# Moving the pool of weight slots to a 512-byte boundary of the storage, and four more dummy products in the router

## The chip, the core and the metric

The kernel runs on one core of a Trainium2 chip. Five engines work side by side on that core's on-chip storage: TensorE (PE in the profile; its weight loads are listed apart as PEld), VectorE (DVE), ScalarE (ACT), GpSimd (POOL) and SyncE (SP), which here only issues transfers. Sixteen DMA engines move data between the chip's main memory and the storage. [...]

The metric is the time of one execution in microseconds (us), the median of several.

## The reference

Two blocks run one after the other on 256 tokens of width 1024, in float32. The first block is adaptive normalization, grouped-query attention and spatial gating, and then an expert-choice feed-forward layer; the second is a latent-attention and sliding-window layer followed by a forgetting-attention layer. The part that matters here is the feed-forward layer of the first block:

```python
def expert_choice_ffn(h, w_router, w1, w3, w2):
    n, d = h.shape[1], h.shape[2]
    cap = CAPACITY_FACTOR * n // N_EXPERTS
    aff = jax.nn.softmax((h @ w_router).astype(jnp.float32), axis=-1)
    gate, idx = lax.top_k(jnp.swapaxes(aff, 1, 2), cap)
    xe = jax.vmap(lambda hb, ib: hb[ib])(h, idx)
    hid = jax.nn.silu(jnp.einsum('becd,edf->becf', xe, w1)) * jnp.einsum('becd,edf->becf', xe, w3)
    ye = jnp.einsum('becf,efd->becd', hid, w2) * gate[..., None].astype(h.dtype)
```

There are 16 experts. Each picks 32 of the 256 tokens (`cap`), and has three matrices of 8 MiB, so 384 MiB of expert weights are read once.

## The kernel before

**Storage.** `body` (L63 on) opens pools that are laid into the storage in the order in which they are opened: `consts` (L71), `big` (L72), `work`. `consts` holds the small tables and `xT` (the running activations, 8 KiB in each of 128 partitions). `big` holds 23 slots of 8 KiB in each partition (`NSLOT`); whatever is large lives in a slot: weight chunks `w`, split halves `hi` and `lo`, activations. In the built program the first slot starts at byte 20,768 of each partition, which is 288 bytes past a multiple of 512, and since a slot is 8,192 bytes every slot starts 288 bytes past such a multiple.

**Loads.** Every weight chunk of 1 MiB goes into one slot. `queue` writes the list of loads down in the order in which they are wanted; `pump` (L252) issues them on SP's queue, one after the other, as long as slots are free (less `keep`, a number that `hold` sets for each stage). A load into a slot waits on SP until the slot's last reader is done, and all loads behind it wait with it. A chunk of an expert's `w1`, `w3` or `w2` is 128 rows of 8 KiB that lie in one piece in the main memory and in the slot; a chunk of `w_in`, `o_w_in`, `w_out` and the like is 1,024 pieces of 1 KiB.

**The router, and what follows it.** All engines run their instructions in the order of the program text. After the output projection (`p_out`) TensorE computes router scores (`p_rl`) and sums of squares (`p_st`); VectorE makes the scale; then the softmax, a transpose (`p_af`), and the choice of 32 tokens for each expert, four rounds of three instructions on VectorE (L981 to L984). From the indices a one-hot matrix is built through a small product (`one_hots`: `diag` on VectorE, `p_ix` on TensorE, `oh` on VectorE). For expert 0, `before_first` gathers its tokens chunk by chunk with narrow products (`p_g`, 32 columns) between the products of `hidden` (`p_h`), which read the chunks of `w1` (first pass, k = 0 to 7) and then those of `w3` (second pass). Then `expert` does the second product (`p_y`) and adds the result back to `xT` (`p_sc`). After expert 0 the tokens of the other 15 experts are gathered at once (`p_g`, 480 columns, 32 records), and experts 1 to 15 follow. All products go through the helper at L134.

**Dummy products.** `busy(n)` (L885) multiplies `ones` with `xT` n times into a bank of its own that nobody reads. In the router it stands at two places: `busy(6)` (L955), ahead of the transpose `p_af`, and `busy(9)` (L977), between `p_yn` and `p_ix`, while VectorE chooses the tokens:

```python
    rows_out(3)
    free(yT_)
    busy(9)
    gv = small("gv", (16, 32), bufs=1)
    iv = small("iv", (16, 32), U32, bufs=1)
    for r in range(4):
        V.max(gv[:, 8 * r:8 * r + 8], afT)
        V.max_index(iv[:, 8 * r:8 * r + 8], gv[:, 8 * r:8 * r + 8], afT)
        if r < 3:
            V.match_replace(afT, gv[:, 8 * r:8 * r + 8], afT, -1.0)
```

Of the kernel before, what the change touches and what calls it, by code (L numbers as in the profile page):

```python
# [9 lines left out]
F32 = mybir.dt.float32  # L10
# [53 lines left out]
def body(ctx, tc, x, c, ctx_in, c_ctx, w_mod, b_mod, g_mix, g_ffn, w_in, q_gain, k_gain, v_gain,  # L64
# [3 lines left out]
    nc = tc.nc  # L68
    PE, V, S, G = nc.tensor, nc.vector, nc.scalar, nc.gpsimd

    consts = ctx.enter_context(tc.tile_pool(name="consts", bufs=1))  # L71
    big = ctx.enter_context(tc.tile_pool(name="big", bufs=1))  # L72
    work = ctx.enter_context(tc.tile_pool(name="work", bufs=1))
    psum = ctx.enter_context(tc.tile_pool(name="psum", bufs=1, space=bass.MemoryType.PSUM))
    dram = ctx.enter_context(tc.tile_pool(name="dram", bufs=1, space=bass.MemoryType.DRAM))
# [26 lines left out]
    def bank(name):  # L102
        n = banks_free.popleft()
        t = psum.tile([128, 512], F32, name=name, tag="P%d" % n)
        owner[id(t)] = (banks_free, n, t, name)
        return t

    def free(*ts):
        for t in ts:
            q, n, _, _ = owner.pop(id(t))  # L110
            q.append(n)
        pump()
# [14 lines left out]
    def small(name, shape, dt=F32, bufs=2):  # L127
        return work.tile(list(shape), dt, name=name, tag="sm_" + name, bufs=bufs)
# [4 lines left out]
    def mm(o, lhsT, rhs, start, stop):  # L133
        PE.matmul(o, lhsT, rhs, start=start, stop=stop, skip_group_check=True)  # L134
# [750 lines left out]
    def busy(n):  # L885

        if n:
            p = bank("p_busy")
            for _ in range(n):
                mm(p[:, 0:256], ones, xT[:, 0, :], True, True)  # L890
            free(p)
# [82 lines left out]

    rows_out(3)
    free(yT_)
    busy(9)  # L977
    gv = small("gv", (16, 32), bufs=1)
    iv = small("iv", (16, 32), U32, bufs=1)
    for r in range(4):  # L980
# [914 lines left out]
```

## Time and profile before

| | |
|---|---|
| median of 3 runs | 1402.29 us (1401.91 to 1405.15) |
| the profiled execution's own time | 1401.61 us |
| its span, first to last instruction | 1399.8 us |
| mean granted clock of TensorE | 0.854 |
| TensorE busy | 1094.4 us (78%) |
| VectorE busy | 450.3 us (32%) |
| ScalarE busy | 265.6 us (19%) |
| GpSimd busy | 113.7 us (8%) |
| bytes moved | 482.74 MB, 345 GB/s on the mean |

The busy shares are averages over stages with different limits. From about 250 to 1,119 us the experts' weights stream in; before that stand the first block's attention and the router, and after it the second block. The profile's slices (40 equal ones of 35 us), the chain of waits and the windows tell which limit holds where.

### The profile page before, as it was taken

Reading aid. Unit: us, or ns where it says so; the run is one execution under the profiler, and the core shown is the slowest. Engines: PE = TensorE matmul, PEld = TensorE weight load, DVE = VectorE, ACT = ScalarE, POOL = GpSimd, SP = SyncE. Lnnn points to the kernel's source line nnn. Section 1 sums busy time; section 2 is a strip of 40 time slices with the busy share of each in tenths; the row PEclk is TensorE's granted clock in tenths of the full one; section 3 lists DMA queues with packets and bytes.
Section 4 is the critical chain, followed back from the end, with each engine's and each line's share of the span. In section 5 each row is a group of like instructions: output and inputs, shape, how many; then the busy total and the mean of one; then the engine's idle time right before and its main releaser. Section 6 shows DMA issues by size and latency. Waiting matters only on the chain.

```text
span 1399.8 us, 16525 instructions
## 1 busy us (share of the span) xinstructions
PE 1094.4 (78%) x6685; PEld 516.1 (37%) x6685; DVE 450.3 (32%) x1096; ACT 265.6 (19%) x529; POOL 113.7 (8%) x65
## 2 busy tenths in 40 slices
PE   5999998976777676786767767676676878899988
PEld 2775943311111011110101111011110566799877
DVE  3747433201011010110101011010111568967984
ACT  3446310000000000000000000000000345555453
POOL 1000100000000000000000000000000332560420
PEclk9999969968778798877968879687897899999999
DMA  9995799999999999999999999999999971482320
GB/s 371 374 395 238 290 343 412 372 420 420 419 420 420 419 419 420 420 420 419 420 420 420 420 420 420 419 420 419 420 420 415 344 230 61 124 264 84 121 91 31
DMA packets 114684, 482.74 MB, mean 345 GB/s; under 512 B 8010, under 2 KB 61520, under 8 KB 63152
## 3 DMA queue, kind: packets, MB, share of 16 engines
q1 hardware_dynamic: 113504, 479.10, 85.9%
q0 software_dynamic: 848, 2.48, 0.5%
q8 instruction: 53, 0.87, 0.3%
q14 instruction: 23, 0.19, 0.0%
q10 hardware_dynamic: 256, 0.10, 0.0%
HBM read 480.59 MB, written 1.06 MB: 344 GB/s over the span
## 4 chain that ended last, share of the span: by engine, by line
DMA 59%; PE 18%; DVE 9%; issue 2%; ACT 2%; SPq 0%; DVEq 0%; ACTq 0%
DMA w<-in_w_dram 58%; PE p_aT L134 3%; PE p_h L134 2%; PE p_out L134 2%; PE p_oo L134 2%; PE p_g L134 2%; PE p_eo L134 1%; PE p_aN L134 1%; PE p_y L134 1%; DVE pr L1316 1%; PE p_gate L134 1%; DVE pr L1297 1%; DMA w<-in_e_w_in_dram 1%; DVE ogl L1383 1%; PE p_busy L134 1%
## 5 line engine op out<-in xcount | busy, mean ns | idle before, releaser
L134 PE MATMUL p_h<-w,xe 128*32 128x512 f32 x1920 | 356.0, 837 | 179.3 <-DMA w<-in_w_dram 179.3
L134 PE MATMUL p_y<-w,hidT 128*32 128x512 f32 (+1 forms) x1088 | 227.8, 622 | 64.6 <-DMA w<-in_w_dram 46.2
L134 PEld LDWEIGHTS p_h<-w,xe 128*32 128x32 f32 x1920 | 46.7, 125 | 469.6 <-DMA w<-in_w_dram 422.7
L1054 DVE TENSOR_TENSOR hid<-s,p_h 128x512 f32<-128x512 f32 x16 | 11.0, 688 | 506.8 <-issue 454.9
L161 POOL TENSOR_TENSOR lo<-w,hi 128x2048 fp32r<-128x2048 f32 (+2 forms) x20 | 87.0, 4354 | 1024.9 <-DMA w<-in_w_dram 924.2
L134 PEld LDWEIGHTS p_y<-w,hidT 128*32 128x32 f32 x1088 | 53.1, 115 | 246.0 <-issue 174.3
L1067 ACT ACTIVATE ysh<-p_y,ig 128x512 fp32r<-128x512 f32 (+1 forms) x34 | 22.3, 663 | 547.2 <-PE p_y L134 547.2
L1068 DVE SCALAR_TENSOR_TENSOR ysl<-p_y,ig,ysh 128x512 fp32r<-128x512 f32 (+1 forms) x34 | 24.3, 719 | 251.2 <-ACT ysh L1067 249.8
L160 ACT CAST hi<-w 128x2048 fp32r<-128x2048 f32 (+3 forms) x48 | 79.1, 1673 | 25.0 <-DMA w<-in_e_w_in_dram 20.6
L161 DVE TENSOR_TENSOR lo<-w,hi 128x2048 fp32r<-128x2048 f32 (+2 forms) x28 | 52.4, 1893 | 27.2 <-ACT hi L160 25.9
L1052 ACT ACTIVATE s<-p_h 128x512 f32<-128x512 f32 x16 | 9.6, 597 | 265.2 <-PE p_h L134 265.2
L1072 DVE SCALAR_TENSOR_TENSOR xT<-p_sc,m,xT 128x256 f32<-128x256 f32 x128 | 51.8, 475 | 4.0 <-PE p_sc L134 4.0
L134 PE MATMUL p_aT<-y2h,hi 128*128 128x256 f32 x128 | 36.7, 286 | 0.0
L134 PE MATMUL p_aT<-y2h,lo 128*128 128x256 f32 x128 | 36.3, 284 | 0.2 <-POOL lo L161 0.2
L134 PE MATMUL p_aT<-y2l,hi 128*128 128x256 f32 x128 | 36.3, 284 | 0.1
L1301 ACT ACTIVATE pr<-pr,st 128x128 f32<-128x128 f32 x64 | 28.5, 446 | 32.4 <-DVE st L1297 32.4
L134 PE MATMUL p_mod<-w,cm 128*32 128x512 f32 x192 | 27.9, 669 | 3.0 <-DMA w<-in_w_mod_dram 2.2
L1316 DVE TENSOR_SCALAR pr<-pr,st 128x128 f32<-128x128 f32 x64 | 27.4, 490 | 0.6
L134 PEld LDWEIGHTS p_aT<-y2h,hi 128*128 128x128 f32 x128 | 24.5, 191 | 1.0 <-issue 1.0
L134 PE MATMUL p_sc<-oh,ysh 128*128 128x256 f32 x128 | 22.5, 295 | 3.0 <-ACT ysh L1067 3.0
L134 PEld LDWEIGHTS p_aT<-y2h,lo 128*128 128x128 f32 x128 | 24.5, 192 | 0.4 <-POOL lo L161 0.4
L134 PEld LDWEIGHTS p_aT<-y2l,hi 128*128 128x128 f32 x128 | 24.5, 192 | 0.4 <-DVE y2l L1151 0.4
(475 smaller groups left out, 1676.4 us busy)
## 6 DMA issues: line engine op xcount, KB each, us to landing
w<-in_w_dram SPq DMA_DIRECT2D x376, 1024.0 KB, 19.9
w<-in_w_mod_dram SPq DMA_DIRECT2D x24, 1024.0 KB, 11.7
w<-in_o_w_in_dram SPq DMA_DIRECT2D x16, 1024.0 KB, 8.4
w<-in_w_dram SPq DMA_DIRECT2D x16, 512.0 KB, 9.1
w<-in_w_in_dram SPq DMA_DIRECT2D x7, 1024.0 KB, 17.6
w<-in_e_w_in_dram SPq DMA_DIRECT2D x7, 1024.0 KB, 11.7
w<-in_w_out_dram SPq DMA_DIRECT2D x4, 1024.0 KB, 12.6
w<-in_e_w_out_dram SPq DMA_DIRECT2D x4, 1024.0 KB, 11.6
```

The lines of the kernel that those rows point to most:

```text
L134: PE.matmul(o, lhsT, rhs, start=start, stop=stop, skip_group_check=True)
L160: S.copy(r_(hi[:, c_]), t[:, c_])
L161: eng.tensor_tensor(r_(lo[:, c_]), t[:, c_], hi[:, c_], op=OP.subtract)
L1052: S.activation(s1, hp[0], AF.Silu)
L1054: V.tensor_tensor(hid, s1, hp[1], op=OP.mult)
L1067: S.activation(r_(h), yp, AF.Copy, scale=g)
L1068: V.scalar_tensor_tensor(r_(l), yp, g, h, op0=OP.mult, op1=OP.subtract)
L1072: V.scalar_tensor_tensor(xT[:, m, :], p, gt2[:, m:m + 1], xT[:, m, :], op0=OP.mult, op1=OP.add)
L1297: V.tensor_tensor_reduce(t[:, c0:c1], sp[:, c0:c1], bb[b], scale, init, OP.add, OP.min, st[:, 2 * z + b:2 * z + b + 1])
L1301: S.activation(t[:, c0:c1], t[:, c0:c1], AF.Exp, bias=st[:, 2 * z + b:2 * z + b + 1], scale=-1.0, accum_out=st[:, 4 + 2 * z + b:5 + 2 * z ...
L1316: V.tensor_scalar(t[:, c0:c1], t[:, c0:c1], st[:, 8 + 2 * z + b:9 + 2 * z + b], None, op0=OP.mult)
L1383: later.append(lambda: V.tensor_tensor(r_(l[:, i, :]), t, h[:, i, :], op=OP.subtract))
```

## The change

A pool `edge` is opened first, with one tile of 96 floats (384 bytes) in each partition that nothing reads or writes, then `big`, then `consts`. In the built program the first slot then starts at byte 2,560, which is five times 512, and so every slot starts at a multiple of 512; the constants and `xT` lie behind the slots. And the second call of `busy` in the router makes 13 dummy products in the place of 9.

```diff
+    edge = ctx.enter_context(tc.tile_pool(name="edge", bufs=1))
+    edge.tile([128, 96], F32, name="edge")
+    big = ctx.enter_context(tc.tile_pool(name="big", bufs=1))
     consts = ctx.enter_context(tc.tile_pool(name="consts", bufs=1))
-    big = ctx.enter_context(tc.tile_pool(name="big", bufs=1))
     work = ctx.enter_context(tc.tile_pool(name="work", bufs=1))
...
     rows_out(3)
     free(yT_)
-    busy(9)
+    busy(13)
     gv = small("gv", (16, 32), bufs=1)
```

The rows of VectorE, ScalarE, GpSimd and SP are the same in both programs but for line numbers and buffer numbers, and each load goes to the slot that it had. TensorE's rows differ at one place. Before, in the router, between the second `p_yn` (the last two columns of token rows) and `p_ix` (the product that spreads the indices):

```order
520 L968 MATMUL p_af<-ident,lg 16x128 x2
521 L912 MATMUL p_yn<-ident,yT 128x128 x4
522 L134 MATMUL p_busy<-xT,ones 128x256 x9
523 L134 MATMUL p_ix<-diag,ones 128x32
524 L134 MATMUL p_g<-oh_1785,yn 128x32 x4
525 L134 MATMUL p_h_1795<-w_991,x_1784 32x512 x4
```

The same place on TensorE in the changed program (its lines are three further down):

```order
520 L971 MATMUL p_af<-ident,lg 16x128 x2
521 L915 MATMUL p_yn<-ident,yT 128x128 x4
522 L137 MATMUL p_busy<-xT,ones 128x256 x13
523 L137 MATMUL p_ix<-diag,ones 128x32
524 L137 MATMUL p_g<-oh_1793,yn 128x32 x4
525 L137 MATMUL p_h_1803<-w_995,x_1792 32x512 x4
```

Nothing has moved past anything: the row of dummy products ahead of `p_ix` is four longer.

## Rows read from the trace of the kernel before

**Rows 1.** The page: granted clock (tenths) and transfer rate, 40 slices; chain by line.

```profile
PEclk9999969968778798877968879687897899999999
...
GB/s 371 374 395 238 290 343 412 372 420 420 419 420 420 419 419 420 420 420 419 420 420 420 420 420 420 419 420 419 420 420 415 344 230 61 124 264 84 121 91 31
...
DMA w<-in_w_dram 58%; PE p_aT L134 3%; PE p_h L134 2%; PE p_out L134 2%; PE p_oo L134 2%; PE p_g L134 2%; PE p_eo L134 1%; PE p_aN L134 1%; PE p_y L134 1%; DVE pr L1316 1%; PE p_gate L134 1%; DVE pr L1297 1%; DMA w<-in_e_w_in_dram 1%; DVE ogl L1383 1%; PE p_busy L134 1%
```

**Rows 2.** Chain of waits, 171 to 255 us: start, us, what.

```profile
174.70 4.28 PE p_busy L134 x12
...
185.40 0.19 DVE diag L991
...
186.44 1.08 PE p_g L134 x8
...
189.41 1.87 PE p_h L134 x8
191.28 0.99 PE p_g L134 x4
...
203.72 3.57 PE p_h L134 x16
...
207.61 7.83 PE p_h L134 x64
...
232.66 15.01 PE p_g L134 x32
247.67 3.26 PE p_h L134 x29
250.93 12.47 DMA w<-in_w_dram
```

**Rows 3.** Windows from the router on: length, each engine's busy us (records), clock, DMA.

```profile
175.00:180.00 5.00, 5.00 (x20) 4.06 (x19) 2.59 (x13) 1.34 (x6) 0.00 (x0) 0.66 1.02 413
180.00:185.00 5.00, 3.52 (x17) 2.75 (x15) 4.66 (x18) 0.26 (x1) 0.00 (x0) 1.00 1.01 421
185.00:190.00 5.00, 3.96 (x26) 2.41 (x30) 1.74 (x9) 0.29 (x1) 0.00 (x0) 0.87 0.37 111
190.00:215.00 25.00, 25.00 (x142) 8.29 (x134) 3.33 (x13) 2.75 (x5) 0.00 (x0) 0.62 0.98 365
245.00:250.00 5.00, 5.00 (x31) 1.76 (x33) 0.72 (x1) 0.81 (x2) 0.00 (x0) 1.00 0.35 93
250.00:1090.00 840.00, 596.35 (x3024) 121.66 (x3020) 100.14 (x254) 30.02 (x46) 0.00 (x0) 0.80 1.01 419
```

**Rows 4.** SP's waits, 185 to 250 us: total us, times, longest us.

```profile
SPq L252 <- PE p_h L134: 29.0, 16, 8.5
SPq L252 <- PE p_g L134: 14.4, 1, 14.4
```

**Rows 5.** TensorE's timeline: start, us, tile, shape, records [idle before, what ended it].

```profile
179.47 4.05 PE L134 MATMUL p_busy<-xT,ones 128*128 128x256 f32 x18
185.63 0.40 PE L134 MATMUL p_ix<-diag,ones 16*128 16x32 f32 x2 [2.12 <-DVE diag L991]
...
229.82 1.96 PE L134 MATMUL p_ix<-diag,ones 16*128 16x480 f32 x2 [2.69 <-DVE diag L991]
...
1169.46 0.76 PE L1323 MATMUL p_pt<-ident,pr 128*128 128x128 f32 x4 [2.37 <-DVE pr L1316]
...
1332.77 0.93 PE L134 MATMUL p_s<-k,q 64*128 64x128 f32 x8 [2.48 <-DVE k L1698]
```

**Rows 6.** Windows around three of these pauses, columns as in rows 3.

```profile
1165.00:1175.00 10.00, 6.63 (x54) 5.46 (x53) 9.35 (x28) 4.55 (x16) 4.23 (x1) 1.00 0.27 92
1330.00:1340.00 10.00, 7.52 (x67) 6.95 (x64) 9.96 (x26) 4.61 (x13) 4.62 (x1) 1.00 0.32 107
229.00:236.00 7.00, 5.30 (x6) 2.01 (x7) 2.23 (x4) 0.00 (x0) 0.00 (x0) 0.54 1.01 421
```

**Rows 7.** Transfers of 300 to 800 us: packets by size.

```profile
DMA packets 28801, 209.88 MB, mean 420 GB/s; under 512 B 3195, under 2 KB 3195, under 8 KB 3195
```

**Rows 8.** Transfers of 1240 to 1260 us, loads in pieces of 1 KiB.

```profile
DMA packets 6923, 7.00 MB, mean 350 GB/s; under 512 B 111, under 2 KB 6921, under 8 KB 6921
```

## The prediction

> **What bounds the kernel now.** I read the page first. Its chain by line [rows 1] gives 58% of the span to transfers of the experts' weights and no other line more than 3%; its transfer rate stands at 419 or 420 GB/s from slice 9 to slice 30, and nowhere else so long. The windows say the same of that stage in one row: from 250 to 1,090 us the DMA engines are busy throughout (share 1.01) at 419 GB/s, while TensorE is busy 596 of 840 us at a mean clock of 0.80 [rows 3]. So in this stage the time is bytes over rate, and TensorE's speed is worth nothing there.
>
> The stage's beginning is another matter. The chain in order of time [rows 2] runs through TensorE and VectorE until 250.93 us and only then through transfers. Up to there the loads wait for TensorE to release slots: the transfer rate is 111 GB/s from 185 to 190 us, 365 from 190 to 215 and 93 from 245 to 250, beside 421 in the neighbouring 180 to 185 [rows 3]. SP's waits name the cause: 29.0 us in 16 waits for `p_h` of expert 0 (each frees a chunk), and one of 14.4 us for the big gather `p_g`, which ends at 247.67 us [rows 2, 4]. Whatever brings TensorE earlier to the end of that gather lets the stream start earlier, until the stream itself has no hole left.
>
> In this stretch TensorE's clock falls. It is 1.00 from 180 to 185 us, 0.87 from 185 to 190 and 0.62 on the mean from 190 to 215 [rows 3]. Ahead of the fall TensorE finished nine dummy products at 183.52 us and then sat idle for 2.12 us, until `diag` let it start `p_ix` [rows 5]; what follows until 187.52 us is `p_ix` and eight records of the narrow `p_g` [rows 2]. So for 4.0 us, from 183.52 to 187.52, it did nothing wide.
>
> **The change part by part: four more dummy products.** Nine take 4.05 us [rows 5], so one takes 0.45 us at the upper level and four take 1.80 us. They lie in the idle 2.12 us before `p_ix`, which waits for VectorE either way: the run ends at 179.47 + 13 × 0.45 = 185.32 us, and `diag` ends at 185.59 us [rows 2]. Queued behind them on TensorE is `p_ix`, and behind that everything of expert 0; the cover left is 0.27 us, so their own cost is nothing, and if the cover were gone each would cost 0.45 us.
>
> What they may change is the clock. The stretch without a wide product shrinks from 4.0 us to 187.52 − 185.32 = 2.2 us. Two pauses of TensorE of about that length lie elsewhere in this trace, 2.37 us before 1,169.46 and 2.48 us before 1,332.77 [rows 5], and the clock around both stays at 1.00 [rows 6]. A longer one, 2.69 us before 229.82 us [rows 5], comes with a clock of 0.54 [rows 6]. The new stretch lies on the side of the two. I take it that the clock stays at the upper level.
>
> Then expert 0's first pass runs faster. At the lower level eight records of `p_h` take 1.87 us and four of `p_g` 0.99 us; at the upper level 64 of `p_h` take 7.83, so eight take 0.98, and eight of `p_g` take 1.08, so four take 0.54 [rows 2]. Until 207.3 us there are six of those groups of `p_g` (the first partly at the upper level), five groups of eight `p_h` and one of sixteen in 3.57 us. Gain: 6 × (0.99 − 0.54) + 5 × (1.87 − 0.98) + (3.57 − 1.96) = 2.7 + 4.45 + 1.6 = 8.8 us for TensorE.
>
> Not all of that reaches the end, since the stream becomes the limit. The holes that it can close are 25 × (1 − 365/421) = 3.3 us from 190 to 215 us and 5 × (1 − 93/421) = 3.9 us from 245 to 250 us [rows 3], together 7.2 us. The hole between 185 and 190 us remains: it ends when the first `p_h` of expert 0 is done, at 188.5 us, which the dummies don't move. The smaller of 8.8 and 7.2 counts: **−7.2 us**. If the clock falls all the same, the term is 0.
>
> **The change part by part: the slots' place.** It adds and removes no instruction. It changes where each row of a load begins in the storage, and of the engines' operands only addresses; no row before shows a load into a slot that begins at a multiple of 512, so I bound it. In the saturated half millisecond [rows 7] 28,801 − 3,195 = 25,606 packets of 8 KiB passed through 16 engines in 500 us, 312.4 ns each. In the stretch of loads in pieces of 1 KiB [rows 8], 6,921 − 111 = 6,810 such packets passed in 20 us, 47.0 ns each. The line through both has 37.9 ns for each KiB and a remainder of 9.1 ns that does not grow with size. Where a row begins can only touch that remainder: the bytes are the same. The stage holds 840 × 419 GB/s / 1.0486 MB = 336 loads of 1 MiB, each with 8 packets for each engine, so 1 ns of a packet is 336 × 8 ns = 2.7 us. The upper end of the gain is the whole remainder, 9.1 × 2.7 = 24.5 us, which would need a packet without any setup. A loss isn't excluded by anything here; its nearest row is the spread of the saturated slices, 419 to 420 GB/s, 0.24% or 2.0 us [rows 1]. I take a tenth of the remainder, 0.9 ns: **−2.4 us**. It is near the low end because the nearest rows, the saturated slices themselves, look like steady streaming with hardly any slack. Elsewhere I count nothing: from 171 to 250 us the chain has no load in it [rows 2], and while the first three slices move 371 to 395 GB/s [rows 1], they hold some 38 loads only, a ninth of the stage's.
>
> [...]
>
> **Sum.** Against the profiled execution's own 1,401.6 us (span 1,399.8 and 1.8 around it): 1401.6 − 7.2 − 2.4 = 1392.0. The median of the runs lies 0.7 us above that execution, so the forecast for the median is **1392.7 us**, 0.7% faster.
>
> **The rivals.** *The clock falls all the same.* Against the two pauses that cost nothing stands that the 2.2 us end in narrow work, and that after 171 us TensorE was busy without a break [rows 2] on narrow products and the clock still stood at 0.66 from 175 to 180 [rows 3]. Also the first pass of expert 0 alternates narrow and wide groups, and once low the clock stayed low for about 20 us. Then only the place counts: 1402.3 − 2.4 = 1399.9, and between 1394 and 1404 if the place gives 8 or costs 2. That is also the case in which the change does not do what it says.
>
> *The place is worth more.* If a third of the remainder goes, 3.0 ns, it is 8.2 us for 2.4, and with the clock held 1402.3 − 7.2 − 8.2 = 1386.9. For it speaks that the DMA engines are the limit for 840 us, so that every nanosecond of a packet counts 2,690 times; against it that nothing in the rows shows such a cost.
>
> *The dummies run at the lower level, slower than before.* The clock is at 0.66 from 175 to 180 us and the first six dummies, on the chain, took 4.28 us there [rows 2, 3], for 6 × 0.45 = 2.7 at the upper level. If that low stretch comes some 3 us later, or lasts on, the 13 dummies run at 0.90 us each: 179.47 + 11.7 = 191.2 us, 5.5 us after `diag` is ready, and `p_ix`, expert 0 and the stream all start that much later. The time would be 1402.3 + 5.5 − 2.4 = 1405.4, or 1407.8 if the place gives nothing. It decides from 0.54 us of the lower level under the dummies, which lengthens them by half of that, the 0.27 us of cover. The rows speak against it: from 180 to 185 us the clock is at 1.00 [rows 3], with the first six dummies right ahead.
>
> **How the numbers follow.** Clock held and the place worth little: 0.60. Clock falls all the same: 0.22. The place worth more, with the clock held: 0.09. Dummies at the lower level, or the place a loss without the clock's gain: 0.09. About 0.3% (4.2 us) is what a measurement of this kernel can tell from no change. Faster by more, below 1398.1: the first and third cases, 0.69, and a fifth of the second, 0.04, so 0.73. Within: the rest of the second, 0.18. Slower: 0.09. The range reaches from a little below the third case's 1386.9, 1385, to the end of the second without any gain, 1402.5, so **1385 to 1402.5**; the likeliest case's own is 1387 to 1397, from a gain of the place of 8 us to a loss of 2.
>
> **What would show it.** Right: a TensorE timeline without a pause ahead of `p_ix`, with `p_ix` still released by `diag` 6.2 us after the dummies begin; a clock of 1.00 from 185 us on until past 205; `p_h` of the first pass in groups of 0.98 us; no hole in the transfer rate around the end of the big gather, which ends near 239 us. For the place: packets of 8 KiB below 312.4 ns and a rate above 420 GB/s in the saturated stage. Wrong: `p_h` still at 1.87 us in the first pass, a saturated rate that has not moved, or a `p_ix` that waits for the dummies.

## The result and the profile after

The changed kernel takes **1384.06 us** (median of 4 runs, 1381.31 to 1386.54) beside 1403.49 for the kernel before in the same session: ratio 0.9861, 95% interval 0.9833 to 0.9889. Forecast were 1392.7 us and a range of 1385 to 1402.5. The sign was right; the time lies 0.9 us below the range. Its four runs are not spread evenly: 1381.31 and 1381.92, then 1386.19 and 1386.54; below they are called the lower and the upper group. The median lies between the two, where no run lies: the upper pair is inside the range, the lower pair 3 to 4 us below it. The execution that was profiled is one of the upper pair (1386.19 us, span 1384.4), 15.4 us below the profiled one of before.

The page of after, clock and transfer rate in 40 slices [rows 1]:

```profile
PEclk9999968978778787887968878587886989999999
...
GB/s 377 401 403 212 283 343 419 369 427 427 427 427 427 427 426 427 427 427 427 427 427 426 427 427 427 427 427 427 426 427 415 369 183 81 107 289 62 123 91 31
```

The plateau of the weights' stream stands at 426 or 427 GB/s, where it was 419 or 420. The windows of after (length, busy us of PE, PEld, DVE, ACT and POOL with records, granted clock, DMA share, GB/s) say where nothing changed [rows 3]:

```profile
175.00:180.00 5.00, 5.00 (x22) 4.12 (x22) 2.63 (x12) 1.28 (x5) 0.00 (x0) 0.77 1.00 419
180.00:185.00 5.00, 4.55 (x22) 3.60 (x20) 4.10 (x17) 0.00 (x0) 0.00 (x0) 1.00 0.94 398
185.00:190.00 5.00, 4.65 (x28) 2.15 (x28) 1.27 (x6) 0.29 (x1) 0.00 (x0) 0.75 0.36 79
190.00:215.00 25.00, 24.29 (x138) 8.30 (x134) 3.90 (x14) 2.74 (x5) 0.00 (x0) 0.64 1.00 379
245.00:250.00 5.00, 5.00 (x40) 1.49 (x42) 0.71 (x1) 0.66 (x1) 0.00 (x0) 1.00 0.46 141
250.00:1090.00 840.00, 601.91 (x3117) 130.78 (x3110) 109.27 (x262) 35.20 (x55) 5.12 (x3) 0.80 1.01 425
```

The clock, which the dummies were to hold, falls in this execution as it did before: a mean of 0.64 from 190 to 215 us. The granted clock is a share of full speed, and its records in the traces of before and of after hold two values only, 1.00 and 0.50, the upper and the lower level; from 190 to 205 us of after it reads 0.50 throughout, from 205 to 210 a mean of 0.70, from 210 to 215 1.00. The hole in the transfers around 245 to 250 us is still there (141 GB/s). The chain of waits of after, start and us [rows 2]:

```profile
173.60 4.28 PE p_busy L137 x12
...
184.30 0.19 DVE diag L994
...
188.35 1.87 PE p_h L137 x8
...
231.57 15.00 PE p_g L137 x32
246.56 3.22 PE p_h L137 x29
249.79 12.16 DMA w<-in_w_dram
```

`p_h` of the first pass still goes at 1.87 us for eight, and the gather ends at 246.56 us, 1.1 us earlier than before. Those 1.1 us were there already at the first `p_busy` (173.60 for 174.70), ahead of the dummies. The timeline of TensorE shows that the dummies did what they could: the idle time ahead of `p_ix` is 0.39 us for 2.12 [rows 5], and `diag` still releases it.

```profile
184.54 0.40 PE L137 MATMUL p_ix<-diag,ones 16*128 16x32 f32 x2 [0.39 <-DVE diag L994]
185.35 1.08 PE L137 MATMUL p_g<-oh,yn 128*128 128x32 f32 x8 [0.41 <-DVE oh L999]
```

SP waits for the same as before [rows 4]:

```profile
SPq L255 <- PE p_h L137: 29.4, 17, 8.5
SPq L255 <- PE p_g L137: 14.3, 1, 14.3
```

So in this execution all but about 1 us of the gain comes after 250 us, from the stream. The transfers of 300 to 800 us of after [rows 7]:

```profile
DMA packets 29284, 213.40 MB, mean 427 GB/s; under 512 B 3250, under 2 KB 3250, under 8 KB 3250
```

29,284 − 3,250 = 26,034 packets of 8 KiB through 16 engines in 500 us are 307.3 ns each, for 312.4 before: 5.1 ns less. In the second block a stretch of loads in pieces of 1 KiB, 1,225 to 1,230 us of after [rows 8]:

```profile
DMA packets 1915, 1.93 MB, mean 386 GB/s; under 512 B 32, under 2 KB 1915, under 8 KB 1915
```

1,915 − 32 = 1,883 packets in 5 us are 42.5 ns each, for 47.0: 4.5 ns less. A packet of an eighth of the size saves nearly the same, so what went is a cost that hardly grows with the packet's bytes.

### The profile page after: what moved, and what is told of

Read it like the earlier page. It is cut to its first block, busy times and chain, and to the rows that moved or that the text cites. A ratio compares the mean times of both kernels' runs of the same rounds, so it can differ in the third digit from the quotient of the medians.

```text
span 1384.4 us, 16541 instructions
## 1 busy us (share of the span) xinstructions
PE 1089.4 (79%) x6693; PEld 521.6 (38%) x6693; DVE 449.8 (32%) x1096; ACT 265.6 (19%) x529; POOL 113.4 (8%) x65
## 4 chain that ended last, share of the span: by engine, by line
DMA 58%; PE 18%; DVE 9%; issue 2%; ACT 2%; SPq 0%; DVEq 0%; ACTq 0%
DMA w<-in_w_dram 58%; PE p_aT L137 3%; PE p_h L137 2%; PE p_out L137 2%; PE p_oo L137 2%; PE p_g L137 2%; PE p_eo L137 1%; PE p_aN L137 1%; DVE pr L1319 1%; PE p_y L137 1%; PE p_gate L137 1%; DMA w<-in_e_w_in_dram 1%; DVE pr L1300 1%; DVE ogl L1386 1%; PE p_busy L137 1%
## 5 line engine op out<-in xcount | busy, mean ns | idle before, releaser
L137 PE MATMUL p_h<-w,xe 128*32 128x512 f32 x1920 | 348.2, 820 | 178.3 <-DMA w<-in_w_dram 178.3
L137 PEld LDWEIGHTS p_aT<-y2h,hi 128*128 128x128 f32 x128 | 24.5, 192 | 1.0 <-issue 1.0
L137 PEld LDWEIGHTS p_aT<-y2h,lo 128*128 128x128 f32 x128 | 24.5, 192 | 0.4 <-POOL lo L164 0.4
L137 PEld LDWEIGHTS p_aT<-y2l,hi 128*128 128x128 f32 x128 | 24.5, 192 | 0.3 <-DVE y2l L1154 0.3
```

## The experiments

Theory: the time is the sum of two parts, the place of the slots (about −16 us in every run) and the clock in expert 0's first pass (about −5 us in the runs in which the four dummies hold it). Rivals: that the order of the pools, not the start address, matters; that the two groups of runs have nothing to do with the clock; that an earlier end of the gather can't be used by the stream. Times of before are from the same chip in each group.

### Each part alone

The place without the dummies, against the changed kernel:

```diff
-    busy(13)
+    busy(9)
```

> The slots moved, but nine dummy products as before. Theory A (the start address alone pays): the saturated rate is 427 GB/s as in the changed kernel, the 8 KiB packets take 307.5 ns of an engine, and the time is about 15 us below the kernel before (ratio about 0.989), with all of the clock's fall in the first pass of expert 0. Theory B (the dummies pay a good part, in those runs in which they hold the clock): the ratio stays at about 0.989 and no run comes near 1381 us, so the changed kernel's two runs at 1381 to 1382 are the dummies' doing. Theory C (the dummies pay nothing, the spread is chance): the runs spread over 1381 to 1387 us as in the changed kernel.

Measured: 1386.79 us median of 6 runs (five from 1386.38 to 1388.45, one at 1396.04), ratio to before 0.9894 (0.9869 to 0.9919); before 1402.67. None near 1381, and in the profiled one the clock from 190 to 215 us is 0.59. The transfers of 300 to 800 us, in the form of [rows 7]:

```profile
DMA packets 29290, 213.42 MB, mean 427 GB/s; under 512 B 3253, under 2 KB 3253, under 8 KB 3253
```

The whole step from 420 to 427 GB/s comes with the place: −15.9 us.

The dummies without the place, against the kernel before:

```diff
-    busy(9)
+    busy(13)
```

> Thirteen dummy products, the slots where they were. Theory A: rate 420 GB/s, time as before within 2 us (ratio 0.999 to 1.001). Theory B: in some runs the clock holds through the first pass of expert 0 and the time is about 5 us below, so that the runs fall into two groups, near 1402 and near 1397 us (ratio about 0.998). The first forecast had 7.2 us in each run (ratio 0.995).

Measured: 1402.09 us median of 12 runs, ratio 0.9988 (0.9974 to 1.0001), rate unchanged at 420 GB/s. Three of the twelve took 1395.89, 1397.62 and 1398.98; of the 17 runs of before beside it none was below 1400.97. In the profiled execution (1401.32 us) the clock from 190 to 215 us is 0.62, as before:

```profile
190.00:215.00 25.00, 25.00 (x142) 8.31 (x134) 3.34 (x13) 2.74 (x5) 0.00 (x0) 0.62 0.97 362
```

Taken alone, the four dummies change most runs by nothing, and a few by 4 to 7 us. The highest of the three does not stand clear: a run of before in another group took 1399.62.

### Order of the pools, or start address

The slots first in the storage as in the change, but 288 bytes past a multiple of 512, as they were before (start 2,336), thirteen dummies:

```diff
-    edge.tile([128, 96], F32, name="edge")
+    edge.tile([128, 40], F32, name="edge")
```

> The slots lie first, as in the changed kernel, but each begins 288 bytes past a multiple of 512 as in the kernel before; 13 dummies. Theory A (the start address): rate 420 GB/s, 8 KiB packets at 312.5 ns, time about 1401 us. Rival D (the order of the pools, or the place of the constants, pays): rate 427 GB/s, time about 1386 us.

Measured: 1403.72 us in one run.

```profile
DMA packets 28805, 209.89 MB, mean 420 GB/s; under 512 B 3199, under 2 KB 3199, under 8 KB 3199
```

And the other way, the order of before with a pad of 224 bytes between constants and slots, so that these begin at 20,992, a multiple of 512 (against the kernel before, with thirteen dummies):

```diff
     consts = ctx.enter_context(tc.tile_pool(name="consts", bufs=1))
+    edge = ctx.enter_context(tc.tile_pool(name="edge", bufs=1))
+    edge.tile([128, 56], F32, name="edge")
     big = ctx.enter_context(tc.tile_pool(name="big", bufs=1))
```

> The constants lie first, as in the kernel before, and 224 unused bytes behind them make each slot begin at a multiple of 512; 13 dummies. Theory A (the start address): rate 427 GB/s, 8 KiB packets at 307.5 ns, time about 1385 us. Rival D (the order of the pools): rate 420 GB/s, time about 1401 us.

Measured: 1386.26 us in one run.

```profile
DMA packets 29288, 213.39 MB, mean 427 GB/s; under 512 B 3255, under 2 KB 3255, under 8 KB 3255
```

The rates settle it: which pool comes first pays nothing, and the start address alone pays all. In both runs the clock fell (0.64 from 190 to 215 us), so their times are without the dummies' part.

### Which multiple

The changed kernel with four other starts, by the size of the `edge` tile alone (without it for 128 past):

```diff
-    edge.tile([128, 96], F32, name="edge")
+    edge.tile([128, 32], F32, name="edge")     start 2,304: 256 past
or
+    edge.tile([128, 112], F32, name="edge")    start 2,624: 64 past
or
+    edge.tile([128, 104], F32, name="edge")    start 2,592: 32 past
```

> The changed kernel with its slots moved back by 256 bytes: they begin at byte 2,304, a multiple of 256 and not of 512. Theory 256 (what counts is a multiple of 256, or of something smaller): rate of the saturated half millisecond 427 GB/s, some 29,290 packets, time 1381 to 1388 us. Theory 512 (the start must be a multiple of 512, or the gain is from the slots' place in another sense that only multiples of 512 share): 420 GB/s, some 28,800 packets, 1396 to 1404 us. [...]

> The changed kernel with its slots at byte 2,176, 128 past a multiple of 256. Theory 256 (a row that does not begin at a multiple of 256 costs one more piece, whatever the remainder): 420 GB/s and 1396 to 1404 us, as at 32 past. Theory grain (the cost depends on a smaller power of two, 64 or 128 bytes): 427 GB/s and 1381 to 1388 us. A graded cost would show as a rate between 421 and 426.

> The changed kernel with its slots at byte 2,624, 64 past a multiple of 512. Theory 256: 420 GB/s, 1396 to 1404 us. Theory grain of 64: 427 GB/s, 1381 to 1388 us; grain of 128: 420 GB/s. With the run at 128 past it tells 64, 128 and 256 apart.

> The changed kernel with its slots at byte 2,592, 32 past a multiple of 512, where the kernel before has them 288 past. Every theory on the start address has 420 GB/s and 1396 to 1404 us here, unless only the half of the 512 bytes in which the start lies matters: then 427 GB/s and 1381 to 1388 us.

Measured, one run each beside 1402.62 of before, the transfers of 300 to 800 us in this order, 256, 128, 64 and 32 past:

```profile
DMA packets 29290, 213.40 MB, mean 427 GB/s; under 512 B 3256, under 2 KB 3256, under 8 KB 3256
```

```profile
DMA packets 28907, 210.65 MB, mean 421 GB/s; under 512 B 3209, under 2 KB 3209, under 8 KB 3209
```

```profile
DMA packets 28901, 210.60 MB, mean 421 GB/s; under 512 B 3209, under 2 KB 3209, under 8 KB 3209
```

```profile
DMA packets 28795, 209.86 MB, mean 420 GB/s; under 512 B 3193, under 2 KB 3193, under 8 KB 3193
```

| start | ns per 8 KiB packet | time, us |
|---|---|---|
| multiple of 256 | 307.3 | 1385.78 |
| 128 past | 311.3 | 1398.79 |
| 64 past | 311.4 | 1398.70 |
| 32 past | 312.5 | 1402.65 |

The clock fell in all four (0.62 or 0.63 from 190 to 215 us), so the times compare; but they are single runs, and 4 us is not much more than runs of one kernel spread, so the packets carry the reading. A multiple of 256 is enough; 512 buys nothing more (307.3 ns at both). Past that the cost is nearly whole at once, 4.0 ns at 128 or 64, with 1.1 ns more at 32.

### The clock held

One more dummy between `p_ix` and the first narrow `p_g` of expert 0, against the changed kernel; then two there:

```diff
     one_hots(0, 1, oh0)
+    busy(1)
```

```diff
     one_hots(0, 1, oh0)
+    busy(2)
```

> The changed kernel with one more dummy product between p_ix and the first narrow p_g of expert 0, so that no wide product is missing for the whole way from the thirteen dummies to the first p_h. Theory clock (the fall at about 190 us is what separates the two groups of runs of the changed kernel, 1381 and 1386 us): the clock stands at 1.00 from 185 us to past 205, the first pass of p_h runs in groups of 0.98 us, the gather ends some 7 us earlier, and all runs lie near 1381, 5 us below the upper group. Rival (the stream cannot use an earlier end of the gather): the same clock, and runs at 1386. Rival (one product is too little): the clock falls at 190 us, runs in two groups as before, plus 0 to 0.5 us.

> As the run with one dummy product there, with two: 0.45 us each at the upper level, of which the first p_g waits for at most 0.9 us. Theory clock: clock 1.00 from 185 to past 205 us, all runs near 1381. Rival (stream): the clock held and runs at 1386. Rival (too little): the clock falls, two groups of runs, plus 0 to 0.9 us.

Measured: one, 1381.97 us (5 runs, 1380.06 to 1382.74), ratio 0.9842 (0.9817 to 0.9867); two, 1381.37 us (6 runs, five from 1380.85 to 1381.67, one at 1387.15), ratio 0.9849 (0.9824 to 0.9875); before 1402.83. Ten of eleven runs lie in the lower group. The windows of the run with one, and its chain:

```profile
190.00:215.00 25.00, 23.68 (x206) 8.01 (x198) 5.67 (x20) 2.74 (x5) 0.00 (x0) 1.00 0.99 395
215.00:245.00 30.00, 25.54 (x122) 11.20 (x122) 9.46 (x17) 3.99 (x7) 0.00 (x0) 0.94 1.01 427
245.00:250.00 5.00, 5.00 (x52) 1.56 (x48) 0.00 (x0) 0.51 (x1) 0.00 (x0) 1.00 1.01 428
```

```profile
186.73 0.63 PE p_busy L137 x2
187.36 0.85 PE p_g L137 x8
...
237.84 2.76 PE p_h L137 x24
240.62 17.30 DMA w<-in_w_dram
```

The clock is at its upper level from 190 to 215 us (1.00) and most of the time to 245 (0.94), no hole is left around 245 us, and the chain goes over to the transfers at 240.62 us for 249.79.

The same one dummy with the slots in their old place (the kernel before, with `busy(13)` and `busy(1)`):

> The kernel before, slots in their old place, with thirteen dummies and one more between p_ix and the first narrow p_g. Theory clock: the clock is held as in the runs with the bridge and the new place, 1.00 from 190 to 215 us, and the gain is that of those runs against place alone, 4 to 7 us: 1395 to 1399 us in all runs, rate 420 GB/s. Rival (the held clock pays only where the stream is faster): 1401 to 1403 us with the clock held. Rival (not held): two groups, 1396 to 1399 and 1401 to 1404.

Measured: 1396.43 us (5 runs, 1395.59 to 1397.20), ratio 0.9952 (0.9938 to 0.9965); before 1402.98. The rate of 300 to 800 us is 420 GB/s, and the windows have

```profile
190.00:215.00 25.00, 22.82 (x199) 7.82 (x198) 5.58 (x20) 3.49 (x7) 0.00 (x0) 1.00 0.99 403
245.00:250.00 5.00, 5.00 (x52) 1.56 (x48) 0.00 (x0) 0.00 (x0) 0.00 (x0) 1.00 1.01 419
```

The held clock alone is worth **−6.5 us** (4.9 to 8.7 by the interval). Against [rows 3] its transfers gain 25 × (403 − 365)/420 = 2.3 us and 5 × (419 − 93)/420 = 3.9 us in these two windows, some 6 together, which is the prediction's arithmetic of holes with measured ends. Of the three low runs of the dummies alone, one (1395.89) lies among its runs; the others lie 0.4 and 1.8 us above the highest of them, so that their clock held is likely and not shown.

### The changed kernel again, and nine dummies with the one behind

> The changed kernel once more, for the spread of its runs alone. Theory clock: two groups again, some runs at 1381 to 1382.5 and some at 1386 to 1387, since whether the clock falls at about 190 us differs from run to run; in the profiled one the clock from 190 to 215 us is 1.00 if its time is 1381 to 1382.5, and 0.6 if it is 1386 or more. Rival: both groups with the same clock there, or only one group; then the four dummies have no part in the difference.

Measured, nothing changed: 1380.99 us median of 4 runs (1379.97, 1380.41, 1381.57 and 1385.30), ratio 0.9851 (0.9834 to 0.9869). This time the profiled execution is one of the lower group (1380.41 us). Its timeline, windows and chain, to be laid beside those of after above:

```profile
184.39 0.40 PE L137 MATMUL p_ix<-diag,ones 16*128 16x32 f32 x2 [0.39 <-DVE diag L994]
```

```profile
175.00:180.00 5.00, 4.20 (x24) 3.44 (x23) 3.24 (x16) 1.27 (x5) 0.00 (x0) 1.00 1.02 424
190.00:215.00 25.00, 22.77 (x195) 8.08 (x192) 6.56 (x21) 3.72 (x6) 0.00 (x0) 1.00 1.00 414
245.00:250.00 5.00, 5.00 (x52) 1.46 (x48) 0.00 (x0) 0.00 (x0) 0.00 (x0) 1.00 1.00 423
```

```profile
187.87 0.99 PE p_h L137 x8
...
221.99 15.15 PE p_g L137 x32
237.14 2.76 PE p_h L137 x24
239.91 16.64 DMA w<-in_w_dram
```

The same program, with the same pause of 0.39 us ahead of `p_ix` and `p_ix` starting within 0.2 us of where it did. From 190 to 215 us the clock is 1.00 for 0.64, `p_h` at 0.99 us for 1.87, the gather's end at 237.14 for 246.56. They already differ from 175 to 180 us, where the clock is 1.00 for 0.77. The two executions are 5.8 us apart. This is the difference between the groups, seen in one program; the other runs are put to a group by their time alone.

Nine dummies as before the change, and the one behind `p_ix`, slots in the new place:

```diff
-    busy(13)
+    busy(9)
...
     one_hots(0, 1, oh0)
+    busy(1)
```

> The changed kernel with nine dummies as before and the one between p_ix and p_g: the pause of 2.12 us ahead of p_ix is back, and then comes one wide product. Theory A (the four are needed as well): the clock falls in some or all runs, runs near 1386 or in two groups. Theory B (one wide product behind the pause is enough): the clock held, all runs at 1380 to 1383 us.

Measured: 1388.52 us median of 5 runs (1381.98 to 1392.20), ratio 0.9882 (0.9863 to 0.9901). One run of five is in the lower group. In the profiled one, which reached the router some 5 us late, TensorE's timeline and the window have

```profile
184.81 4.05 PE L137 MATMUL p_busy<-xT,ones 128*128 128x256 f32 x18
190.97 0.40 PE L137 MATMUL p_ix<-diag,ones 16*128 16x32 f32 x2 [2.11 <-DVE diag L994]
191.31 0.70 PE L137 MATMUL p_busy<-xT,ones 128*128 128x256 f32 x2
```

```profile
190.00:215.00 25.00, 24.03 (x118) 9.72 (x122) 4.11 (x17) 3.03 (x6) 0.00 (x0) 0.59 0.85 313
```

The pause of 2.11 us ahead of `p_ix` is back and one wide product behind it did not repair it there: the clock is down again, 0.59 from 190 to 215 us. The four dummies do have a part; they suffice alone in some runs, and with the one behind `p_ix` in nearly all. In the table the lower group is near 1381 us with the new place and near 1396 with the old.

| kernel | runs in the lower group |
|---|---|
| place alone (nine dummies) | 0 of 6 |
| nine and one behind, new place | 1 of 5 |
| thirteen, old place | 3 of 12, one of them not clear |
| thirteen, the six single runs with other starts or order | 0 of 6 |
| the change (thirteen, new place) | 5 of 8 |
| thirteen and one or two behind, either place | 15 of 16 |

## Why the prediction was right and wrong

**What bounds the kernel** held: the stream's time is bytes over rate, and 1.6% of its rate came out as most of some 16 us, with TensorE's clock there at 0.80 as before.

**The place of the slots is the step that failed.** The method was right and the size was not. Of the remainder of 9.1 ns in a packet the prediction took a tenth, 0.9 ns. It was 5.1 ns, more than half: 5.1 × 2.69 = 13.7 us in the stage for the 2.4 of the sum. The place alone gave 15.9 us, so some 2 us came from what the prediction counted at nothing. The run at 256 past, whose clock fell as before, shows where. These are the transfers from their first start on the chain to the landing of the last expert chunk on it, before and then in that run, from 250.93 to 1,091.20 us and from 250.65 to 1,076.24:

```profile
DMA packets 50452, 351.89 MB, mean 419 GB/s; under 512 B 5398, under 2 KB 7872, under 8 KB 7872
DMA packets 50197, 351.81 MB, mean 426 GB/s; under 512 B 5391, under 2 KB 7593, under 8 KB 7593
```

The same bytes to 0.1 MB took 840.3 and 825.6 us, 14.7 less. Among them are 2,474 and 2,202 pieces of 512 B to 2 KB, loads of the second block, for which the 4.5 ns above make an estimated 0.6 to 0.7 us. The way from there to the first `p_bc` of the second block, before and in that run, is 0.8 us shorter:

```profile
1134.61 1.12 PE p_bc L1276 x4
1118.88 1.12 PE p_bc L1279 x4
```

In the kernel before a load of the second block stood on the chain there for 10.19 us. Before the router nothing sure was gained: the 1.1 us of after are a difference between executions, and in the run with slots at 256 past the first `p_busy` began at 175.1 us, later than before. Nor was any gained behind `p_bc`: it starts 15.7 us earlier in the run at 256 past and 16.6 in after (1,117.97), and the ends lie 15.8 and 15.4 us apart. From there on the chain has no load in it, before and in after, so the faster loads of the second block are hidden by its other work. Drawn anew through 307.3 and 42.5 ns the line has 37.8 ns for each KiB and 4.7 ns remaining, so only the remainder moved, as argued. The bounds of that term, −24.5 to +2.0, held it; the choice inside them did not, and the range was cut at 1385, just below the rival with a third of the remainder. The reason given for the low end, that saturated slices look like steady streaming with hardly any slack, was no reason: the share of the DMA engines was 1.01 from 250 to 1,090 us with packets of 312.4 ns and with packets of 307.3, so an even rate said that the engines were always busy, not what a packet contained. The packet records of the trace of before had more to say: from 300 to 800 us nearly all of their 8 KiB packets last from 309 to 321 ns, 314.8 on the mean, and those of after nearly all last 309. The shortest of before already had the length that all were to have, 5.8 ns below the mean.

**The clock** was right in place and size, and its mechanism was too simple: it was taken as held or lost for all runs at once. Where it held, everything in the prediction's list for it came: `p_ix` released by `diag` with no pause left to speak of, 1.00 to past 205 us, groups of 0.99 us, no hole at the gather's end near 237 us (239 was said). Alone it is worth 6.5 us for the 7.2 in the sum; with the faster stream 5 to 6. But by their times it held in 5 of 8 runs of the changed kernel only. The step behind it, that a stretch of 2.2 us without a wide product lies on the side of the two harmless pauses, is therefore not a yes or no: in the two profiled executions of one program it once fell and once did not.

**The dummies' own cost** was nothing, as said: the cover ahead of `p_ix` was 0.39 us for the 0.27 worked out. In neither profiled execution did they run late, so the slower rival did not come about. Its 0.90 us for a dummy at the lower level is near the trace of before, where one took 0.85 us at 0.50 (two records, 176.20 to 177.05 us) and 0.43 at 1.00 (two records from 180.12).

**The rivals.** The profiled execution at 1386.19 us is the first of them (the clock falls all the same) with a place worth twice the 8 us at which that case was ended; the lower runs are the second with 5.1 ns for 3.0. By the terms as measured, the sum reads 1402.3 − 15.9 = 1386.4 where the clock falls and, with a further 5 to 6 us, some 1381 where it holds. That is the two groups.

**What stays open.** Why the same program keeps the clock in one execution and loses it in another, and why the thirteen dummies kept it in 5 of 8 runs of the changed kernel and in 3 of 18 of the others (counts this small may differ by chance; the two single runs that started at a multiple of 256 lost it too), no run here shows. The profiled executions give a hint. In all eight with thirteen dummies and none behind in which the clock fell, it had already been down for a while ahead of the thirteen, with a mean of 0.66 to 0.77 from 175 to 180 us; in the one in which it held it was 1.00 there. But in the runs with thirteen and one behind `p_ix` it was 0.66 and 0.70 there, in the new place and in the old, and held all the same. Nor does any run show what the 5.1 ns are spent on.

The kernel with one or two dummies behind `p_ix` is no faster than the lower group of the changed kernel; it is in that group nearly always, ten runs of eleven for five of eight (medians 1381.97 and 1381.37, for 1384.06 and 1380.99 of the changed kernel in its two series).

## What to carry to other kernels

Where a stage is a saturated stream, put the destination rows at a multiple of 256 bytes by a look at the address that the allocator gave, before anything else; a pad costs a few bytes, and here 288 bytes past had 420 GB/s for 427 and cost 1.1% of the whole kernel. When a term has bounds ten times as far apart as the value taken, a price of 2.7 us for each nanosecond, and no row of its own, the range must reach through those bounds. Two lengths of packet in the trace told here what part of it could move, and the spread of packets of one length, from the shortest to the mean, would have told how far. An effect that hangs on the clock is to be forecast as a share of runs, and steadied by closing each pause of wide work rather than one of them: 15 of 16 runs here for 8 of 26.

## What the runs showed of the hardware

- The start of the rows in the core's storage, with source, sizes, queues and instructions the same, sets the rate of loads of 8 KiB rows: 427 GB/s at a multiple of 256, 421 at 64 or 128 past, 420 at 32 or 288 past.
- The cost is nearly the same for a packet of 1 KiB (4.5 ns) as for one of 8 KiB (5.1 ns), so short rows pay more: 386 GB/s for 350 in the stretches of 1 KiB pieces, 10%, of which little reached the time here.
- With the same program, the same pause of 0.39 us ahead of `p_ix`, and `p_ix` starting 0.15 us apart, TensorE's granted clock from 190 to 215 us was 0.64 in one execution and 1.00 in another.
